# Weight sums of a Strassen-Winograd feed-forward: three VectorE operations a pair ahead instead of four GpSimd ones, and two products copied by ScalarE

## The chip, the cores and the metric

The kernel runs on one core of a Trainium2 chip. A core has TensorE (PE in the rows; its weight loads are PEld), VectorE (DVE), ScalarE (ACT), GpSimd (POOL) and SyncE (SP), which here issues nearly all DMAs. Each engine works through its own queue in order, and engines wait for each other on semaphores. The metric is the device time of one execution in microseconds, less being better, and the median of several runs is what is compared.

## The reference, cut to what matters

A decoder trunk of two layers, 512 tokens, width 1024. The change touches the four half-step feed-forwards alone (two in each layer, hidden width 2816):

```python
def swiglu_ffn(x, w_gu, w_down):
    gate, up = jnp.split(x @ w_gu, 2, axis=-1)
    return (jax.nn.silu(gate) * up) @ w_down
...
for i in range(DEPTH):
    x = x + 0.5 * swiglu_ffn(rmsnorm(x, ffn1_norm[i]), ffn1_w_gu[i], ffn1_w_down[i])
    x = x + Mixer_i(rmsnorm(x, mix_norm[i]))
    x = x + 0.5 * swiglu_ffn(rmsnorm(x, ffn2_norm[i]), ffn2_w_gu[i], ffn2_w_down[i])
```

All of it is float32. The kernel splits every operand in a rounded high part and a low part, and takes each product as high times high, high times low and low times high.

## The kernel before, in words

There are six stages: `f0a` (feed-forward), `ab` (a recurrent mixer), `f0b`, `f1a` (feed-forwards), `nsa` (an attention mixer) and `f1b` (feed-forward). Activations lie feature by token, eight tiles X[0..7] of 128 x 512, and all matmuls have a 128 x 128 weight block that stands still.

**A feed-forward** (`ffn`) has 22 hidden tiles of 128 units, each a *pair* of a gate tile and an up tile. The first four (`CLASSIC`) are taken in the plain way, from the gain-scaled but not yet normalised input `x` (`x phase` below): meanwhile the root mean square is found (`rms_sum`, `rms_row` give `Rcol`, then `R`), and `Quarters` makes the normalised input `xn` and from it seven combinations of its quarters, each split in high and low (`split`): B11, Q7, Q6 in `before()`, B21, Q4, Q5, B22 in `after()`. Their order is that of VectorE's queue.

The other 18 pairs use a Strassen-Winograd scheme, seven half-size products for eight: the gate and the up matrix of a hidden tile are a 2 x 2 block matrix (two halves of the 1024 features), the input another (two halves of the features by two halves of the tokens). `Pair.load` brings 1 MB of weights into two buffers `r` (`ra`, `rc`, four blocks of 128 x 512 each; two such sets, used in turn), forms the four sums of blocks that the scheme wants on GpSimd (lines 301 to 304), and splits the seven blocks in four *parts*: ScalarE copies the high part (`whi` or `wx`, line 310), VectorE subtracts for the low one (`wlo` or `wx`, line 311). There are five part buffers for four parts a pair. `Pair.p1` to `p7` are the products, 12 matmuls of 256 columns each, 84 a pair: product 1 and 7 start a sum in PSUM (`a`, `e`), later ones add on top of it, and after each of them ScalarE or VectorE takes out what stands there, before the next product changes it. In the order of TensorE's queue a pair is p1, p7, then p3 of the pair before, p6, p2, p4, p5. So p3, which adds into the same bank `a` as p5, comes 24 matmuls after p5, and must wait until VectorE has read what p5 left (line 355). `p3` also forms silu(gate) times up (line 362) and its split `h` (lines 380, 381).

Pairs come in groups of 4, 8 and 6 for lack of room for `h`; after each group the down projection (weights `wd`) adds into X. The two first pairs of a stage are interleaved: p.p1, p.p7, p.p6, q.p1, q.p7, p.p2, p.p4, p.p5 and so on.

**What sets the order.** TensorE's order is written out. On the other engines a scheduler places the instructions by priority: code under `tc.high_priority(offset=N)` counts as if written N instructions earlier. `SAHEAD` is the offset of a pair's loads, sums and splits, `EV` that of the PSUM reads, `AHEAD` that of the plainly used weights (`wload`). Once placed, a queue is never reordered when the program runs.

Of the kernel before, what the change touches and what calls it, by code (L numbers as in the profile page):

```python
# [12 lines left out]
P = 128  # L13
T = 512
# [10 lines left out]
SAHEAD = 230  # L25
EV = 320
# [27 lines left out]
def build(tc, a, out, stages=("f0a", "ab", "f0b", "f1a", "nsa", "f1b")):  # L54
    nc = tc.nc
    with ExitStack() as ctx:
# [182 lines left out]
        class Quarters:  # L239
# [12 lines left out]
            def split(self, name, src):  # L252
                t = blk(self.qb[QS.index(name)], F32R, f"q{name}")
                hi, lo = (t[:, n * 4 * H:(n + 1) * 4 * H].rearrange("p (k t) -> p k t", k=4) for n in range(2))
                nc.scalar.activation(hi, src, AF.Copy)
                nc.vector.tensor_sub(lo, src, hi.bitcast(F32))
                self.Q[name] = hi, lo

            def before(self):
                b11, b12, b21, b22 = self.f  # L260
                nc.vector.tensor_sub(b22, b12, b22)
                self.split("B11", b11)
                nc.gpsimd.tensor_sub(b12, b12, b11)
                self.split("Q7", b22)
                nc.vector.tensor_sub(b11, b11, b22)
                self.split("Q6", b11)

            def after(self):
                q6, q5, b21, b22 = self.f
                nc.gpsimd.tensor_add(b22, q5, q6)  # L270
                self.split("B21", b21)
                nc.vector.tensor_sub(b21, b21, q6)
                self.split("Q4", b21)
                self.split("Q5", q5)
                self.split("B22", b22)
# [12 lines left out]
        class Pair:  # L288
# [4 lines left out]
            def load(self, w, rb):  # L293
                with tc.high_priority(offset=SAHEAD):
# [3 lines left out]
                    nc.sync.dma_start(ra[:, 0:4:3], w[0].rearrange("p (s c) -> p s c", s=2))  # L298
                    nc.sync.dma_start(rc[:, 3], w[1][:, :T])
                    nc.sync.dma_start(rc[:, 0], w[1][:, T:])  # L300
                    nc.gpsimd.tensor_sub(ra[:, 1], rc[:, 3], ra[:, 0])  # L301
                    nc.gpsimd.tensor_add(rc[:, 1], rc[:, 0], rc[:, 3])
                    nc.gpsimd.tensor_sub(ra[:, 2], rc[:, 1], ra[:, 0])  # L303
                    nc.gpsimd.tensor_sub(rc[:, 2], ra[:, 3], ra[:, 2])
                    for src, names in ((ra[:, 0:2], ("B11", "Q7")), (ra[:, 2:4], ("Q6", "B21")),
                                       (rc[:, 0:2], ("Q4", "Q5")), (rc[:, 2:3], ("B22",))):
# [16 lines left out]
            def p1(self):  # L323
                self.a, self.t1 = psum(), tp.tile([P, T], F32, name="t1", bufs=3)
                self.product(self.a, "B11", True)
                with tc.high_priority(offset=EV):
                    nc.scalar.activation(self.t1[:, :H], self.a[:, :H], AF.Copy)

            def p2(self):
                b = psum()  # L330
                self.product(b, "B21", True)
                with tc.high_priority(offset=EV):
                    nc.vector.tensor_add(self.t1[:, :H], b[:, :H], self.t1[:, :H])
                nc.scalar.activation(self.t1[:, :H], self.t1[:, :H], AF.Silu)
# [17 lines left out]
            def p5(self):  # L352
                self.product(self.a, "Q5", False)
                with tc.high_priority(offset=EV):
                    nc.vector.tensor_add(self.t2[:, H:], self.a[:, :H], self.t2[:, H:])  # L355

            def p3(self):
                self.product(self.a, "B22", False)
                with tc.high_priority(offset=EV):
                    nc.scalar.activation(self.t1[:, H:], self.a[:, :H], AF.Silu)  # L360
# [4 lines left out]
        def ffn(gname, wgu, wd, x, lay, nxt, first=None):  # L365
# [30 lines left out]
            for j in range(CLASSIC):  # L396
                eng = nc.gpsimd if j > 1 else None
                (gh, gl), (uh, ul) = first if first and j == 0 else (wload(wgu[j, 0], eng=eng),
                                                                     wload(wgu[j, 1], eng=eng))
# [866 lines left out]
```

## Time and profile before

| | us |
|---|---|
| median of three runs | 2122.34 |
| lowest, highest | 2117.0, 2123.83 |
| the profiled execution | 2126.54 |
| its span, first to last instruction | 2124.8 |

The profile is of one execution, 4.2 us over the median; some 1.7 us of it lie outside the span. A row of the timeline has a start, a duration and, in square brackets, how long the engine had been idle and who ended that. Durations of neighbouring rows overlap by some 0.07 us, so that the cost of an instruction in a full queue is the distance between two starts. The clock column (PEclk) is the share of TensorE's 2.4 GHz that was granted; 0.5 is its lower level, 1.2 GHz.

### The profile page before, as it was taken

What the parts mean: (1) busy time and instruction counts of PE and PEld (TensorE: products, weight loads), DVE (VectorE), ACT (ScalarE), POOL (GpSimd) and SP (SyncE); (2) the same over time, 40 slices, a digit from 0 to 9 for tenths busy, and PEclk for the clock granted to TensorE, in tenths of its full rate; (3) what the DMA queues carried; (4) which work ended last, traced back from release to release, by engine and by line L of the source; (5) the groups of instructions that cost most, each with busy time, mean ns of one, the idle gap of its engine ahead of it and who ended that gap; (6) DMA issues with size and microseconds to landing.
All of it is one profiled execution on the core that took longest, in us unless ns stands there. A gap on an engine that the chain in (4) does not pass through costs nothing.

```text
span 2124.8 us, 30587 instructions
## 1 busy us (share of the span) xinstructions
PE 2019.0 (95%) x11896; PEld 1753.4 (83%) x11896; DVE 1432.3 (67%) x2021; ACT 1015.2 (48%) x1828; POOL 858.3 (40%) x602
## 2 busy tenths in 40 slices
PE   7999999989998999999999999999999989999997
PEld 5889889767787889898798989877777667889896
DVE  4957757488658759485866947443877778659474
ACT  4535436445544435254543525434877754435252
POOL 6425523243134427163433614202655554427152
PEclk8999999999899999999999999999999999999998
DMA  4233322222132323233232333321100032323212
GB/s 160 80 110 95 115 75 75 90 80 90 60 99 80 108 81 112 83 101 94 80 110 90 100 94 95 119 84 60 36 16 30 17 114 70 100 90 108 86 61 84
DMA packets 73585, 182.09 MB, mean 86 GB/s; under 512 B 7264, under 2 KB 8032, under 8 KB 73440
## 3 DMA queue, kind: packets, MB, share of 16 engines
q1 hardware_dynamic: 73296, 180.06, 26.7%
q8 instruction: 93, 1.52, 0.3%
q14 instruction: 52, 0.43, 0.1%
q10 hardware_dynamic: 144, 0.09, 0.0%
HBM read 178.02 MB, written 2.10 MB: 85 GB/s over the span
## 4 chain that ended last, share of the span: by engine, by line
PE 75%; DVE 12%; issue 4%; ACT 3%; POOL 3%; DMA 1%; SPq 0%; POOLq 0%; DVEq 0%; ACTq 0%
PE ps L174 18%; PE ps L175 18%; PE ps L176 18%; PE pt L175 3%; PE pt L176 3%; PE pt L174 3%; PE px L977 2%; PE pt L772 2%; DVE wx L311 1%; DVE wlo L169 1%; DMA r<-wgu 1%; PE pt L993 1%; DVE h L381 1%; DVE t L362 1%; DVE wlo L311 1%
## 5 line engine op out<-in xcount | busy, mean ns | idle before, releaser
L301 POOL TENSOR_TENSOR r<-r,r 128x512 f32<-128x512 f32 x72 | 124.0, 1723 | 627.7 <-DMA r<-wgu 587.8
L168 ACT ACTIVATE whi<-raw 128x1024 fp32r<-128x1024 f32 (+2 forms) x196 | 193.2, 987 | 368.9 <-PE ps L175 268.2
L175 PE MATMUL ps<-h,whi 128*128 128x512 f32 x704 | 277.2, 394 | 0.5 <-DVE h L381 0.5
L174 PE MATMUL ps<-h,whi 128*128 128x512 f32 x704 | 276.3, 393 | 0.9 <-ACT h L380 0.9
L176 PE MATMUL ps<-h,wlo 128*128 128x512 f32 x704 | 276.5, 393 | 0.0
L311 DVE TENSOR_TENSOR wlo<-r,whi 128x1024 fp32r<-128x1024 f32 (+1 forms) x174 | 237.2, 1365 | 50.3 <-ACT whi L310 48.9
L310 ACT ACTIVATE whi<-r 128x1024 fp32r<-128x1024 f32 (+1 forms) x174 | 165.5, 951 | 188.5 <-PE ps L175 129.4
L169 DVE TENSOR_TENSOR wlo<-raw,whi 128x1024 fp32r<-128x1024 f32 (+2 forms) x150 | 186.7, 1246 | 76.4 <-ACT whi L168 71.6
L450 DVE SCALAR_TENSOR_TENSOR X<-ps,X 128x512 f32<-128x512 f32 x96 | 66.4, 691 | 253.9 <-PE ps L176 253.9
L169 POOL TENSOR_TENSOR wlo<-raw,whi 128x1024 fp32r<-128x1024 f32 (+1 forms) x46 | 108.7, 2364 | 257.0 <-ACT whi L168 247.5
L311 DVE TENSOR_TENSOR wx<-r,wx 128x1024 fp32r<-128x1024 f32 (+1 forms) x114 | 170.2, 1493 | 57.5 <-ACT wx L310 57.1
L174 PE MATMUL ps<-x,whi 128*128 128x512 f32 x432 | 179.7, 416 | 0.4 <-ACT x L103 0.4
L174 PE MATMUL ps<-qB,whi 128*128 128x256 f32 x520 | 148.5, 286 | 25.0 <-DVE t L355 25.0
L176 PE MATMUL ps<-x,wlo 128*128 128x512 f32 x432 | 171.5, 397 | 0.0
L175 PE MATMUL ps<-x,whi 128*128 128x512 f32 x432 | 171.0, 396 | 0.3 <-DVE x L104 0.3
L175 PEld LDWEIGHTS ps<-h,whi 128*128 128x128 f32 x704 | 132.9, 189 | 31.0 <-DVE h L381 2.3
L174 PEld LDWEIGHTS ps<-h,whi 128*128 128x128 f32 x704 | 133.0, 189 | 30.7 <-ACT h L380 1.8
L176 PEld LDWEIGHTS ps<-h,wlo 128*128 128x128 f32 x704 | 132.8, 189 | 28.6
L115 POOL TENSOR_TENSOR acc<-acc,t 128x512 f32<-128x512 f32 x48 | 74.8, 1558 | 189.4 <-ACT t L113 178.3
L175 PE MATMUL ps<-qB,whi 128*128 128x256 f32 x520 | 146.4, 282 | 0.0
L176 PE MATMUL ps<-qB,wlo 128*128 128x256 f32 x520 | 146.4, 282 | 0.0
L303 POOL TENSOR_TENSOR r<-r,r 128x512 f32<-128x512 f32 x72 | 134.3, 1865 | 5.3
(341 smaller groups left out, 5897.7 us busy)
## 6 DMA issues: line engine op xcount, KB each, us to landing
r<-wgu SPq DMA_DIRECT2D x72, 512.0 KB, 3.9
r<-wgu SPq DMA_DIRECT2D x144, 256.0 KB, 2.8
raw<-wd SPq DMA_DIRECT2D x64, 512.0 KB, 3.5
raw<-wgu SPq DMA_DIRECT2D x30, 512.0 KB, 3.6
raw<-wd SPq DMA_DIRECT2D x32, 384.0 KB, 3.1
raw<-ab_fm SPq DMA_DIRECT2D x21, 512.0 KB, 3.5
raw<-nsa_fm SPq DMA_DIRECT2D x17, 512.0 KB, 3.5
raw<-ab_out SPq DMA_DIRECT2D x8, 512.0 KB, 3.6
```

The lines of the kernel that those rows point to most:

```text
L115: nc.gpsimd.tensor_add(acc, acc, sq)
L168: nc.scalar.activation(hi[:, :n], raw[:, :n], AF.Copy)
L169: (eng or nc.vector).tensor_sub(lo[:, :n], raw[:, :n], hi[:, :n].bitcast(F32))
L174: nc.tensor.matmul(ps, wh, xh, start=start, stop=False, skip_group_check=on)
L175: nc.tensor.matmul(ps, wh, xl, start=False, stop=False, skip_group_check=on)
L176: nc.tensor.matmul(ps, wl, xh, start=False, stop=stop, skip_group_check=on)
L301: nc.gpsimd.tensor_sub(ra[:, 1], rc[:, 3], ra[:, 0])
L303: nc.gpsimd.tensor_sub(ra[:, 2], rc[:, 1], ra[:, 0])
L310: nc.scalar.activation(hi[:, :m], src, AF.Copy)
L311: nc.vector.tensor_sub(lo[:, :m], src, hi[:, :m].bitcast(F32))
L450: nc.vector.scalar_tensor_tensor(X[i], ps, 0.5, X[i], op0=OP.mult, op1=OP.add)
L772: nc.tensor.matmul(p2[m][:, :155].rearrange("p (g n) -> p g n", g=5), w[:, q * 256 + m * P:q * 256 + (m + 1) * P], tt[:, :, n:n + 8 * 30 + ...
```

## The change

- The four sums of a pair become three, all additions, on VectorE: one of 128 x 1024 with an input that is repeated, and two of 128 x 512. Signs are put right elsewhere: the quarters B11, B21 and B22 are split from minus their value, and the silu takes scale -1.
- The loads of a pair (now four of 256 KB instead of one of 512 KB and two of 256 KB) and the sums get an offset of their own, `RAHEAD` = 400; the splits keep 230. The parts hold other names: B11 Q7, B21 Q6, Q5 Q4, B22.
- Two sums of the input quarters and the low parts of the classic weights of hidden tiles 2 and 3 go from GpSimd to VectorE too.
- Product 1 is copied by ScalarE into a second PSUM bank, product 2 adds on top of it, and the silu reads that bank: VectorE's addition after p2 is gone. Product 5 is copied by ScalarE into a tile `u4` (one buffer), and VectorE adds from there.

GpSimd keeps the sums of squares (`acc`) and its work in the two mixers.

```diff
+RAHEAD = 400
...
             def split(self, name, src):
...
-                nc.scalar.activation(hi, src, AF.Copy)
-                nc.vector.tensor_sub(lo, src, hi.bitcast(F32))
+                if name[0] == "B":
+                    nc.scalar.activation(hi, src, AF.Copy, scale=-1.0)
+                    nc.vector.scalar_tensor_tensor(lo, src, -1.0, hi.bitcast(F32), op0=OP.mult, op1=OP.subtract)
+                else:
+                    nc.scalar.activation(hi, src, AF.Copy)
+                    nc.vector.tensor_sub(lo, src, hi.bitcast(F32))
...
-                nc.gpsimd.tensor_sub(b12, b12, b11)
+                nc.vector.tensor_sub(b12, b12, b11)
...
-                nc.gpsimd.tensor_add(b22, q5, q6)
                 self.split("B21", b21)
                 nc.vector.tensor_sub(b21, b21, q6)
                 self.split("Q4", b21)
                 self.split("Q5", q5)
+                nc.vector.tensor_add(b22, q5, q6)
                 self.split("B22", b22)
...
             def load(self, w, rb):
-                with tc.high_priority(offset=SAHEAD):
+                with tc.high_priority(offset=RAHEAD):
...
-                    nc.sync.dma_start(ra[:, 0:4:3], w[0].rearrange("p (s c) -> p s c", s=2))
+                    nc.sync.dma_start(ra[:, 0], w[0][:, :T])
                     nc.sync.dma_start(rc[:, 3], w[1][:, :T])
-                    nc.sync.dma_start(rc[:, 0], w[1][:, T:])
-                    nc.gpsimd.tensor_sub(ra[:, 1], rc[:, 3], ra[:, 0])
-                    nc.gpsimd.tensor_add(rc[:, 1], rc[:, 0], rc[:, 3])
-                    nc.gpsimd.tensor_sub(ra[:, 2], rc[:, 1], ra[:, 0])
-                    nc.gpsimd.tensor_sub(rc[:, 2], ra[:, 3], ra[:, 2])
-                    for src, names in ((ra[:, 0:2], ("B11", "Q7")), (ra[:, 2:4], ("Q6", "B21")),
-                                       (rc[:, 0:2], ("Q4", "Q5")), (rc[:, 2:3], ("B22",))):
+                    nc.sync.dma_start(ra[:, 3], w[1][:, T:])
+                    nc.sync.dma_start(rc[:, 0], w[0][:, T:])
+                    nc.vector.tensor_add(ra[:, 1:3], ra[:, 0:4:3], rc[:, 3:4].to_broadcast([P, 2, T]))
+                    nc.vector.tensor_add(rc[:, 1], ra[:, 0], ra[:, 2])
+                    nc.vector.tensor_add(rc[:, 2], rc[:, 0], rc[:, 1])
+                with tc.high_priority(offset=SAHEAD):
+                    for src, names in ((ra[:, 0:2], ("B11", "Q7")), (rc[:, 0:2], ("B21", "Q6")),
+                                       (ra[:, 2:4], ("Q5", "Q4")), (rc[:, 2:3], ("B22",))):
...
             def p1(self):
-                self.a, self.t1 = psum(), tp.tile([P, T], F32, name="t1", bufs=3)
+                self.a, self.b, self.t1 = psum(), psum(), tp.tile([P, T], F32, name="t1", bufs=3)
                 self.product(self.a, "B11", True)
                 with tc.high_priority(offset=EV):
-                    nc.scalar.activation(self.t1[:, :H], self.a[:, :H], AF.Copy)
+                    nc.scalar.activation(self.b[:, :H], self.a[:, :H], AF.Copy)
             def p2(self):
-                b = psum()
-                self.product(b, "B21", True)
+                self.product(self.b, "B21", False)
                 with tc.high_priority(offset=EV):
-                    nc.vector.tensor_add(self.t1[:, :H], b[:, :H], self.t1[:, :H])
-                nc.scalar.activation(self.t1[:, :H], self.t1[:, :H], AF.Silu)
+                    nc.scalar.activation(self.t1[:, :H], self.b[:, :H], AF.Silu, scale=-1.0)
...
             def p5(self):
                 self.product(self.a, "Q5", False)
+                u4 = tp.tile([P, H], F32, name="u4", bufs=1)
                 with tc.high_priority(offset=EV):
-                    nc.vector.tensor_add(self.t2[:, H:], self.a[:, :H], self.t2[:, H:])
+                    nc.scalar.activation(u4, self.a[:, :H], AF.Copy)
+                    nc.vector.tensor_add(self.t2[:, H:], u4, self.t2[:, H:])
             def p3(self):
                 self.product(self.a, "B22", False)
                 with tc.high_priority(offset=EV):
-                    nc.scalar.activation(self.t1[:, H:], self.a[:, :H], AF.Silu)
+                    nc.scalar.activation(self.t1[:, H:], self.a[:, :H], AF.Silu, scale=-1.0)
...
-                eng = nc.gpsimd if j > 1 else None
-                (gh, gl), (uh, ul) = first if first and j == 0 else (wload(wgu[j, 0], eng=eng),
-                                                                     wload(wgu[j, 1], eng=eng))
+                (gh, gl), (uh, ul) = first if first and j == 0 else (wload(wgu[j, 0]), wload(wgu[j, 1]))
```

**VectorE, the start of the program.** In these rows `r0` and `r1` are a pair's buffers `ra` and `rc`, `raw` a block of plainly used weights, `X` and `x` the input and its low part, and the number is that of the tile. Before, from the first row that works on data, and then the rows around the root mean square (`ms`, `Rcol`):

```order
L104 SCALAR_TENSOR_TENSOR x2_96<-X0_70,prm_78,x0_94 128x512
L1127 TENSOR_TENSOR wlo_114<-raw_112,whi_113 128x128
L1127 TENSOR_TENSOR wlo_117<-raw_115,whi_116 128x128
...
L169 TENSOR_TENSOR wlo_238<-raw_235,whi_237 128x1024
L311 TENSOR_TENSOR wx4_555<-r0_546,wx4_555 128x1024
L169 TENSOR_TENSOR wlo_244<-raw_241,whi_243 128x1024
L311 TENSOR_TENSOR wx3_543<-r1_523,wx3_543 128x512
L142 TENSOR_SCALAR ms_268<-ps_263 128x4
```

The same two places of the change:

```order
L309 TENSOR_TENSOR r0_546<-r0_546,r1_547 128x1024
L309 TENSOR_TENSOR r0_522<-r0_522,r1_523 128x1024
L310 TENSOR_TENSOR r1_547<-r0_546 128x512
L310 TENSOR_TENSOR r1_523<-r0_522 128x512
L311 TENSOR_TENSOR r1_547<-r1_547 128x512
L311 TENSOR_TENSOR r1_523<-r1_523 128x512
L1134 TENSOR_TENSOR wlo_114<-raw_112,whi_113 128x128
...
L170 TENSOR_TENSOR wlo_238<-raw_235,whi_237 128x1024
L170 TENSOR_TENSOR wlo_244<-raw_241,whi_243 128x1024
L170 TENSOR_TENSOR wlo_362<-raw_359,whi_361 128x1024
L143 TENSOR_SCALAR ms_268<-ps_263 128x4
```

The sums of the first two pairs now stand ahead of all work on the input (and their eight loads ahead of the input's in SyncE's queue), and no split of a pair stands directly ahead of the root mean square any more.

**VectorE, within a group of pairs** (the eight-pair group of `f0a`). `wlo`, `wx` are low parts, `t2` the up half with its additions, `h` the split product. Before:

```order
L311 TENSOR_TENSOR wx3_1895<-r1_1879,wx3_1895 128x1024
L355 TENSOR_TENSOR t2_1794<-ps_1778,t2_1794 128x256
L311 TENSOR_TENSOR wx4_1898<-r1_1879,wx4_1898 128x512
L311 TENSOR_TENSOR wlo_2011<-r0_2001,whi_2010 128x1024
L311 TENSOR_TENSOR wlo_2015<-r0_2001,whi_2014 128x1024
L362 TENSOR_TENSOR t2_1794<-t1_1779,t2_1794 128x512
L333 TENSOR_TENSOR t1_1902<-ps_1960,t1_1902 128x256
```

Of the change:

```order
L364 TENSOR_TENSOR t2_1679<-u4_1760,t2_1679 128x256
L319 TENSOR_TENSOR wlo_1783<-r1_1764,whi_1782 128x512
L390 TENSOR_TENSOR h8_430<-t2_1555,h8_430 128x512
L319 TENSOR_TENSOR wlo_1897<-r0_1887,whi_1896 128x1024
L309 TENSOR_TENSOR r0_2011<-r0_2011,r1_2012 128x1024
L319 TENSOR_TENSOR wlo_1901<-r1_1888,whi_1900 128x1024
L310 TENSOR_TENSOR r1_2012<-r0_2011 128x512
L371 TENSOR_TENSOR t2_1679<-t1_1664,t2_1679 128x512
L311 TENSOR_TENSOR r1_2012<-r1_2012 128x512
L357 TENSOR_TENSOR t2_1803<-pt_1802,t2_1803 128x256
```

Line 355, the read of product 5 out of PSUM, is gone from this queue (line 364 reads `u4`), and line 309 stands in it three rows behind the last reader of the buffer that its own load refills: `r1_2012` takes the room of `r1_1764`.

**ScalarE at the same place.** Before, the end of a pair (product 5 isn't read here):

```order
L380 ACTIVATE h8_430<-t2_1671 128x512
L310 ACTIVATE wx3_1895<-r1_1879 128x1024
L334 ACTIVATE t1_1779<-t1_1779 128x256
L310 ACTIVATE wx4_1898<-r1_1879 128x512
L327 ACTIVATE t1_1902<-ps_1901 128x256
```

Of the change:

```order
L341 ACTIVATE t1_1788<-ps_1787 128x256
L318 ACTIVATE wx3_1904<-r1_1888 128x1024
L389 ACTIVATE h8_430<-t2_1679 128x512
L363 ACTIVATE u4_1884<-ps_1786 128x256
L318 ACTIVATE wx4_1907<-r1_1888 128x512
L336 ACTIVATE ps_1911<-ps_1910 128x256
```

The copy of product 5 (line 363) stands behind line 389, which waits for VectorE's line 371 of the pair before.

## Rows read from the trace of the kernel before

**Rows 1.** The page: busy time of an engine, share of the span, instructions.

```profile
PE 2019.0 (95%) x11896; PEld 1753.4 (83%) x11896; DVE 1432.3 (67%) x2021; ACT 1015.2 (48%) x1828; POOL 858.3 (40%) x602
```

**Rows 2.** Windows of the eight groups of 8 and 6 pairs: engines busy (instructions), PEclk, DMA.

```profile
164.30:248.50 84.20, 80.12 (x674) 79.47 (x673) 72.84 (x71) 47.20 (x78) 57.60 (x31) 0.99 0.32 101
...
sum 582.90, PE 559.45 PEld 554.54 DVE 480.96 ACT 323.27 POOL 352.13; mean PE 69.93 PEld 69.32 DVE 60.12 ACT 40.41 POOL 44.02
```

**Rows 3.** Windows of the first two pairs (168 matmuls) of each feed-forward.

```profile
675.20:704.40 29.20, 22.77 (x169) 22.12 (x168) 22.83 (x22) 14.99 (x23) 11.92 (x6) 0.88 0.26 85
...
sum 112.70, PE 90.08 PEld 87.50 DVE 90.68 ACT 61.50 POOL 45.73; mean PE 22.52 PEld 21.88 DVE 22.67 ACT 15.38 POOL 11.43
```

**Rows 4.** Windows: 40 us of a group without a TensorE wait, and 8 us with one.

```profile
200.00:240.00 40.00, 40.00 (x341) 39.79 (x340) 36.28 (x38) 24.39 (x41) 29.44 (x17) 1.00 0.33 106
939.00:947.00 8.00, 6.26 (x40) 6.05 (x39) 6.53 (x7) 3.74 (x7) 3.17 (x3) 0.79 0.20 67
```

**Rows 5.** Waits, TensorE: who was waited for, us in total, times, longest.

```profile
PE ps L174 <- DVE t L355: 33.1, 22, 3.9
PE pt L175 <- DVE qQ L256: 11.6, 4, 4.7
PE pt L149 <- DVE Rcol L130: 10.3, 2, 9.1
```

**Rows 6.** Timeline, TensorE, at product 4 of the first pair of f0b.

```profile
690.89 0.58 PE L175 MATMUL pt<-qQ,wx 128*128 128x256 f32 x1 [4.70 <-DVE qQ L256]
691.27 0.41 PE L176 MATMUL pt<-qQ,wx 128*128 128x256 f32 x1
691.49 0.41 PE L174 MATMUL pt<-qQ,wx 128*128 128x256 f32 x1
```

**Rows 7.** Timeline, VectorE, while GpSimd is idle: 128x512, 128x1024, then 128x256 from PSUM.

```profile
73.52 0.68 DVE L381 TENSOR_TENSOR h<-t,h 128x512 fp32r<-128x512 f32 x1
74.13 1.21 DVE L256 TENSOR_TENSOR qQ<-xn,qQ 128x1024 fp32r<-128x1024 f32 x1
75.26 1.21 DVE L256 TENSOR_TENSOR qB<-xn,qB 128x1024 fp32r<-128x1024 f32 x1
...
91.16 0.41 DVE L355 TENSOR_TENSOR t<-ps,t 128x256 f32<-128x256 f32 x1
91.49 0.68 DVE L311 TENSOR_TENSOR wlo<-r,whi 128x512 fp32r<-128x512 f32 x1
```

**Rows 8.** Timeline, VectorE, the same 128x1024 subtraction a little later.

```profile
84.92 2.28 DVE L256 TENSOR_TENSOR qQ<-xn,qQ 128x1024 fp32r<-128x1024 f32 x1
```

**Rows 9.** Timeline, GpSimd, its sums at that time.

```profile
83.99 2.13 POOL L303 TENSOR_TENSOR r<-r,r 128x512 f32<-128x512 f32 x1
```

**Rows 10.** Timeline, SyncE issues a freed buffer's load; GpSimd starts the sum of it.

```profile
92.19 0.34 SPq L299 DMA_DIRECT2D r<-wgu  x1
...
95.18 1.91 POOL L301 TENSOR_TENSOR r<-r,r 128x512 f32<-128x512 f32 x1 [6.83 <-DMA r<-wgu]
```

**Rows 11.** Windows at the start of the program: the input's loads, and a standstill.

```profile
5.00:10.00 5.00, 4.28 (x16) 3.23 (x16) 2.94 (x6) 4.41 (x10) 1.99 (x2) 1.00 1.00 318
...
35.00:40.00 5.00, 0.00 (x0) 0.00 (x0) 1.86 (x1) 1.73 (x3) 4.92 (x4) 0.78 0.00 0
```

**Rows 12.** Timeline, VectorE, around the first root mean square.

```profile
27.81 1.23 DVE L311 TENSOR_TENSOR wx<-r,wx 128x1024 fp32r<-128x1024 f32 x1 [9.59 <-ACT wx L310]
...
38.14 2.16 DVE L311 TENSOR_TENSOR wx<-r,wx 128x512 fp32r<-128x512 f32 x1 [6.87 <-ACT wx L310]
...
40.49 2.03 DVE L128 SCALAR_TENSOR_TENSOR rt<-Rcol 128x4 f32<-128x4 f32 x1
```

**Rows 13.** Timeline, SyncE, loads of the first two pairs at the start.

```profile
18.87 1.08 SPq L299 DMA_DIRECT2D r<-wgu  x2
```

**Rows 14.** Timeline, VectorE, f0b: first use of R, and the last split before product 4.

```profile
645.28 0.69 DVE L387 TENSOR_TENSOR t<-ps,R 128x512 f32<-128x512 f32 x1 [2.15 <-ACT R L151]
...
689.62 1.21 DVE L256 TENSOR_TENSOR qQ<-xn,qQ 128x1024 fp32r<-128x1024 f32 x1
```

## The prediction

> **What bounds the kernel now.** First the page's busy times [rows 1]: TensorE 95% busy, VectorE 67%, GpSimd 40%. A share over the whole span says little here, so the next view is the windows by stage. The eight groups of 8 and 6 pairs hold 4 x (672 + 504) = 4704 matmuls of 256 columns, and take 582.90 us together [rows 2]. What they would take without a wait is read from 40 us in which TensorE was never idle: 341 matmuls, 117.3 ns each, so 84 of them, a pair, take 9.85 us [rows 4]. 4704 x 117.3 ns = 551.8 us, so 31 us of these groups are lost, 0.56 us a pair. The first two pairs of the four feed-forwards take 112.70 us where 8 x 9.85 = 78.8 would do: 33.9 us lost [rows 3]. Eight more pairs, the rest of the groups of four, I take at the 0.56 us: 4.4 us. Beside the pairs there is a standstill at the start of the program, 35 to 40 us without a matmul [rows 11].
>
> The view of the waits names the causes [rows 5]. The largest, 33.1 us in 22 waits, is TensorE waiting for VectorE's line 355, the read of product 5, before it may add product 3 into the same bank. Then 11.6 us for the splits of the quarters (first pairs), 10.3 us for the first Rcol. A wait costs more than its length: behind the 4.70 us wait at 690.89 the matmuls start 0.22 us apart instead of 0.117 (691.27, 691.49), and over an 8 us window with such a wait the granted clock is 0.79, part of it the lower level of 1.2 GHz [rows 4, 6]. So the bound is TensorE, and what is to be had is about 70 us of waits behind VectorE's queue.
>
> **The change part by part.**
>
> *VectorE within a group.* Alone, a 128x1024 operation costs 1.13 us from start to start, a 128x512 one 0.61, a 256-wide read from PSUM 0.33 [rows 7]. A pair costs it now three splits of 1024 and one of 512, three PSUM reads, the product (line 362) and its split: 3 x 1.13 + 3 x 0.61 + 3 x 0.33 = 6.2 us. In the full window it is busy 36.28 of 40 us, and 40 / 9.85 = 4.06 pairs fit in, so it really needs 8.9 us a pair [rows 4]. The 2.7 us between are GpSimd's doing: the subtraction that lasts 1.21 us alone lasts 2.28 while GpSimd sums weights, and GpSimd's sums stretch as well [rows 7 to 9]. The change adds sums of 1.13 + 2 x 0.61 = 2.35 us and removes one PSUM read, 0.33; the addition from `u4` costs what line 355 cost. New need: 6.2 + 2.35 - 0.33 = 8.2 us, say 8.3 with the chain of the dependent sums. Below the 8.9 of now, and below TensorE's 9.85.
>
> But the sums bring a wait into VectorE's queue. Line 309 needs the loads that refill a buffer whose last reader stands three rows ahead of it. From the end of that reader (92.17) to the sum that GpSimd could start on the new data (95.18) it takes 3.0 us [rows 7, 10]. In the queue two operations stand between, 0.61 + 1.13 = 1.7 us of cover; at about half of the pairs there is only one of 1.13. So 1.3 to 1.9 us of standing, 1.6 taken, and a cycle of 8.3 + 1.6 = 9.9 us, level with TensorE's 9.85. Queued behind it are the split of the next pair (line 319) and line 371. Where VectorE runs ahead, its queue stands anyway at line 319 until TensorE frees a part buffer, and the load arrives in that time; so 9.9 holds only where it is late.
>
> *What TensorE waits for.* Product 3 now needs ScalarE's copy of product 5. ScalarE is busy 24.39 of 40 us [rows 4]. Its copy stands behind line 389, which needs line 371 of VectorE: the old dependence is not cut, it gets longer, but line 371 belongs to the pair before, and p3 comes 24 matmuls, 2.8 us, after p5. Followed through one pair of the new order with these durations, the copy ends some 1 us after p5, 1.7 us to spare. So most of the 31 + 4.4 us goes. I keep 0.15 us a pair for a VectorE as full as TensorE, 10 us over 64 pairs: **-25 us**. Bounds: all of it gone, -35; nothing gone, 0; a loss is the first rival.
>
> *The first two pairs of f0b, f1a, f1b.* From R to the split that product 4 waits for, VectorE's own work is now 25 operations of 512 and 13 of 1024, 25 x 0.61 + 13 x 1.13 = 30 us, and it took 45.5 us (645.28 to 690.8) [rows 14]; the rest is GpSimd and waits. In the new order 27 and 21 stand there (classic weights, quarter sums, two of the pair sums, splits of the next pair): 16.5 + 23.7 = 40.2 us, nothing of it stretched. With some 2 us for one load that line 309 waits for and for ScalarE's copies it is 42, 3.3 us earlier: 3 x 3.3 = **-10 us**. Each may be 5 us off: -25 to +5.
>
> *The start of the program.* Removed: VectorE stood at line 311 until GpSimd had made eight sums one after another (38.14), the root mean square stood behind that (one tiny step of it took 2.03 us beside GpSimd), and TensorE stood some 9 us [rows 5, 12], then ran at the lower clock. Added: eight loads, 2.1 MB, ahead of the input. SyncE takes 0.54 us for each [rows 13], 4.3 us, and at the 318 GB/s of the full queue [rows 11] they take 6.6 us; then VectorE makes both pairs' sums, 2 x 2.35 = 4.7 us, before it splits the first tile of the input, at some 13 us instead of 5.3. TensorE begins its second matmul 7 us later. But its first 48 matmuls were held up by the input's loads and splits anyway; laid out with the durations above, they end 2 to 3 us later than now, the third classic weight is split near 30 us, and Rcol follows at 31 us instead of 43. Sum: +3 for the late start, -9 for the wait, -2 for the clock behind it: **-8 us**. Bounds: -12, and +8 if the late start stays whole and Rcol, now behind that third weight's load, waits as long as before.
>
> *Group ends.* Before the down projection VectorE has also the next two pairs' sums in its queue, ahead of the last `h`. Now these ends cost next to nothing; 12 ends at 0.3 us, **+4 us** (0 to +12). The loads' new split, the signs and the second bank cost nothing: four issues of 0.54 us a pair in a queue that is otherwise idle, copies of the same size, one bank more of five, each bank free before its turn.
>
> Sum: -25 - 10 - 8 + 4 = -39 us on an execution of 2126.5 us (span 2124.8 and 1.7 outside), 2087; the profiled run is 4.2 us above the median of 2122.3, so the median becomes **2083 us**.
>
> **The rivals.**
>
> 1. *VectorE becomes the bound, slower.* In these groups a pair takes 582.9 / 56 = 10.41 us now, so the change loses there as soon as line 309 stands longer than 10.41 - 8.3 = 2.1 us a pair. If a late VectorE finds the loads always just issued, it stands the whole 3.0 us: 11.3 us a pair, 0.9 x 64 = +58 us, with the other terms 2122 + 58 - 14 = 2166; half way, 2140. For it: the cover is 1.1 to 1.7 us only [rows 7, 10]. Against: at 9.9 us there is 0.5 us to spare before the present pace. Here the Trainium skill speaks against the change: "Perfetto Trace Analysis", section "Optimizing Scalar/DVE Operations", advises to take work off a saturated VectorE, to ScalarE or even GpSimd, and adds that the shared read port may spoil the latter. By the first half alone the 2 us a pair that are added would be paid in full, 64 x 2 = 128 us, an estimate, about 2250; the row of 36.28 busy in 40 us agrees on the saturation, but rows 7 to 9 show the second half: GpSimd already takes more from VectorE (2.7 us a pair) than its sums will cost there.
>
> 2. *The wait only passes to ScalarE.* If VectorE runs 2 us late, line 371 holds line 389, and that the copy of product 5: p3 waits as before. The pairs gain nothing: -10 - 8 + 4 = -14, 2108. For it: the spare time is 1.7 us. Against: that needs VectorE late at most pairs.
>
> 3. *The late start stays.* +8 instead of -8: 2099. For it: all loads of the input now queue behind 2.1 MB. Against: the Rcol wait is two thirds GpSimd's sums, which are gone.
>
> 4. *A draw:* VectorE at 10.3 us and starts that gain nothing, about 2118.
>
> **How the numbers follow.** The forecast, 2060 to 2098: 0.55. Rival 2: 0.17, rival 3: 0.08, rival 4: 0.06, rival 1: 0.14. About 0.3%, 6.4 us, is what a measurement here can tell from no change: under 2116 is faster, so 0.55 + 0.17 + 0.08 = 0.80 faster, 0.06 the same, 0.14 slower. The range goes from all pair waits and most of the first pairs' gone (-25 to -35 in the groups, -25 at the first pairs, -12, 0: some 2050) up to 2128, which takes in rivals 2 to 4 and the mild end of the first.
>
> **What would show it.** In the profile after: no GpSimd row in the pair groups, and every 1024-wide VectorE row there at 1.2 us (else the 2.7 us were not GpSimd's); idle time before line 309 that ends by a load, 1.3 to 1.9 us where VectorE is late; TensorE's wait for product 5's read down from 33.1 us to under 10, now named after line 363; the eight groups' sum near 560 us; the first row of Rcol near 31 us, and the first split of the input near 13. Wrong if line 309 idles over 2 us at most pairs, if its repeated input makes it slower than 1.21 us, or if the splits of the first pairs come later than before.

## The result, and the profile after

The changed kernel takes 2097.2 us (median of 4 runs, 2094.8 to 2106.2) where the kernel before takes 2123.1: a ratio of 0.9886, 95% interval 0.9854 to 0.9917. That is faster by 26 us; 39 had been forecast, with a range of 2050 to 2128. A second measurement of the changed kernel, made later (below), gave 2105.2 us and 0.9921 [0.9907, 0.9935], so the gain is 18 to 26 us. The sign held and the time lies in the range, but it did not come from where the forecast had put it.

The profiled execution took 2106.2 us, span 2104.5, against 2126.5 and 2124.8 before; it lies 9 us above its own median, which matters below where traces are set against medians. The busy times of the page (columns as in [rows 1]):

```profile
PE 2014.4 (96%) x11896; PEld 1750.7 (83%) x11896; DVE 1383.4 (66%) x2189; ACT 1027.8 (49%) x1900; POOL 280.0 (13%) x290
```

GpSimd has lost 578 us of work. VectorE has 168 operations more and is nevertheless busy 49 us less. TensorE is about as busy as before, and the end moved by 20 us only. Where, the windows tell. The eight groups of 8 and 6 pairs, as [rows 2] (us; PE, PEld, DVE, ACT, POOL busy; granted clock; DMA share):

```profile
158.60:244.40 85.80, 80.34 (x674) 79.70 (x673) 65.67 (x87) 48.00 (x86) 0.00 (x0) 0.98 0.30 92
...
sum 587.70, PE 562.69 PEld 557.27 DVE 434.84 ACT 330.20 POOL 1.55; mean PE 70.34 PEld 69.66 DVE 54.36 ACT 41.28 POOL 0.19
```

587.7 us against 582.9: nothing was won here, where the forecast had put most of the 25 us of its largest term, although VectorE's busy time fell from 481 to 435 us. The groups of four pairs, with which each feed-forward begins, take 183.3 us against 199.5 (matmuls from the first to the last; their first two pairs 100.9 against 112.8), and the first of them begins at 66.4 instead of 71.5. The first two pairs of f0b, as [rows 3], where the kernel before took 29.20 us:

```profile
668.80:695.00 26.20, 22.64 (x170) 22.11 (x169) 18.69 (x22) 13.30 (x22) 0.00 (x0) 0.87 0.14 41
```

TensorE's waits, as [rows 5]:

```profile
PE ps L175 <- ACT u L363: 14.5, 12, 3.1
PE pt L175 <- ACT qQ L261: 8.2, 3, 3.6
PE ps L177 <- DVE wx L319: 7.5, 6, 1.5
...
PE ps L176 <- DVE x L105: 4.9, 3, 1.7
PE pt L176 <- DVE qQ L262: 4.8, 4, 1.5
PE ps L175 <- ACT t L352: 4.6, 2, 3.1
```

The 33.1 us behind product 5 [rows 5] have become 14.5, under the name of ScalarE's copy, and beside them stand new waits for splits of the weights (`wx`) and for the copy of product 6 (line 352). And in the page's costliest groups (busy, mean ns of one, then idle time before and its releaser) there is a row that did not exist:

```profile
L309 DVE TENSOR_TENSOR r<-r,r 128x1024 f32<-128x1024 f32 x72 | 89.4, 1242 | 130.5 <-DMA r<-wgu 130.4
```

VectorE stands 130 us in front of the first sum of a pair, for a load. One such case on VectorE (start, length; in brackets the idle time before and what ended it):

```profile
204.06 1.23 DVE L309 TENSOR_TENSOR r<-r,r 128x1024 f32<-128x1024 f32 x1 [2.50 <-DMA r<-wgu]
...
209.95 0.68 DVE L319 TENSOR_TENSOR wx<-r,wx 128x512 fp32r<-128x512 f32 x1
210.55 0.68 DVE L390 TENSOR_TENSOR h<-t,h 128x512 fp32r<-128x512 f32 x1
211.15 1.22 DVE L319 TENSOR_TENSOR wlo<-r,whi 128x1024 fp32r<-128x1024 f32 x1
214.90 1.23 DVE L309 TENSOR_TENSOR r<-r,r 128x1024 f32<-128x1024 f32 x1 [2.53 <-DMA r<-wgu]
```

and SyncE's issues of the loads meanwhile:

```profile
209.72 0.33 SPq L305 DMA_DIRECT2D r<-wgu  x1
210.09 0.43 SPq L307 DMA_DIRECT2D r<-wgu  x1
210.66 0.34 SPq L306 DMA_DIRECT2D r<-wgu  x1
211.04 0.43 SPq L308 DMA_DIRECT2D r<-wgu  x1
```

The split at 209.95 is the last reader of the pair's second buffer. SyncE issues its loads as soon as it ends (210.63). Behind it VectorE has 1.7 us of work, then it stands 2.53 us until the load of line 306 is there, 4.2 us after its issue. From one line 309 to the next are 10.84 us, 8.31 of work and 2.53 of standing, where TensorE needs 9.85 for a pair [rows 4].

### The profile page after: what moved, and what is told of

Read it like the earlier page. It is cut to its first block, busy times and chain, and to the rows that moved or that the text cites. A ratio compares the mean times of both kernels' runs of the same rounds, so it can differ in the third digit from the quotient of the medians.

```text
span 2104.5 us, 30561 instructions
## 1 busy us (share of the span) xinstructions
PE 2014.4 (96%) x11896; PEld 1750.7 (83%) x11896; DVE 1383.4 (66%) x2189; ACT 1027.8 (49%) x1900; POOL 280.0 (13%) x290
## 4 chain that ended last, share of the span: by engine, by line
PE 72%; DVE 12%; DMA 6%; issue 5%; ACT 3%; POOL 0%; SPq 0%; DVEq 0%; POOLq 0%; ACTq 0%
PE ps L175 17%; PE ps L176 17%; PE ps L177 17%; DMA r<-wgu 6%; PE pt L176 3%; PE pt L175 3%; PE pt L177 3%; PE px L984 2%; PE pt L779 2%; DVE wlo L319 1%; PE pt L1000 1%; DVE wx L319 1%; DVE r L309 1%; DVE r L310 1%; PE ps L944 1%
## 5 line engine op out<-in xcount | busy, mean ns | idle before, releaser
L170 DVE TENSOR_TENSOR wlo<-raw,whi 128x1024 fp32r<-128x1024 f32 (+2 forms) x166 | 192.5, 1162 | 78.7 <-ACT whi L169 73.8
L457 DVE SCALAR_TENSOR_TENSOR X<-ps,X 128x512 f32<-128x512 f32 x96 | 66.4, 691 | 238.1 <-PE ps L177 238.1
L319 DVE TENSOR_TENSOR wlo<-r,whi 128x1024 fp32r<-128x1024 f32 (+1 forms) x174 | 189.1, 1088 | 28.1 <-ACT whi L318 27.8
L309 DVE TENSOR_TENSOR r<-r,r 128x1024 f32<-128x1024 f32 x72 | 89.4, 1242 | 130.5 <-DMA r<-wgu 130.4
L319 DVE TENSOR_TENSOR wx<-r,wx 128x1024 fp32r<-128x1024 f32 (+1 forms) x114 | 125.1, 1098 | 23.6 <-ACT wx L318 21.1
L389 ACT ACTIVATE h<-t 128x512 fp32r<-128x512 f32 x88 | 55.4, 630 | 145.3 <-DVE t L371 143.1
L318 ACT ACTIVATE wx<-r 128x1024 fp32r<-128x1024 f32 (+1 forms) x114 | 107.5, 943 | 11.4 <-DVE r L309 9.1
```

Of the source, the lines that this page charges most:

```text
L170: (eng or nc.vector).tensor_sub(lo[:, :n], raw[:, :n], hi[:, :n].bitcast(F32))
L309: nc.vector.tensor_add(ra[:, 1:3], ra[:, 0:4:3], rc[:, 3:4].to_broadcast([P, 2, T]))
L318: nc.scalar.activation(hi[:, :m], src, AF.Copy)
L319: nc.vector.tensor_sub(lo[:, :m], src, hi[:, :m].bitcast(F32))
L389: nc.scalar.activation(hh, t2, AF.Copy)
L457: nc.vector.scalar_tensor_tensor(X[i], ps, 0.5, X[i], op0=OP.mult, op1=OP.add)
```

## Experiments

Each kernel was timed in three rounds or more beside the kernel before, whose median lay between 2120.3 and 2123.9 us in these sessions; of two kernels from different sessions a difference of some 3 us is therefore not shown. The theory after the first look was that the groups' gain was lost at line 309, and nowhere else; its rivals were ScalarE's copy of product 5 (rival 2 of the prediction) and that VectorE has simply too much to do.

**Line 309 later in the queue.** A one-column copy out of the third split of the pair before, into the place that line 309 overwrites, puts line 309 behind that split. Nothing else changes in the code; the scheduler places the rest of VectorE's queue anew around it.

```diff
-            def load(self, w, rb):
+            def load(self, w, rb, prev=None):
...
+                    if prev is not None:
+                        nc.vector.tensor_copy(ra[:, 1, 0:1], prev.W["Q5"][1][:, 0:1].bitcast(F32))
                     nc.vector.tensor_add(ra[:, 1:3], ra[:, 0:4:3], rc[:, 3:4].to_broadcast([P, 2, T]))
```

> Edit: line 309 of a pair is put later in VectorE's queue, behind the split of products Q5 and Q4 of the pair before (a one-column copy out of that split into the place line 309 overwrites, 0.06 to 0.16 us a pair); loads and all else as in the changed kernel (2097 us). Between the last reader of the buffer and line 309 there now lie some 5 us of VectorE's work instead of 1.1 to 1.7. Theory A (the gain of the groups was lost at line 309, where a load takes 4.3 us from the buffer's release to the sum): VectorE's idle time before line 309 falls from 130 us to under 40, the eight groups from 588 us to about 563, the time to 2070 to 2078. Theory B (ScalarE's copy of product 5 holds product 3, whatever line 309 does): the idle time goes, but TensorE's wait for the copy stays at 10 to 15 us and the groups above 580, time 2090 to 2098. Theory C (VectorE's sums are simply too much work): the idle time moves to other lines, time 2095 to 2105.

Measured: 2040.8 us (2039.1 to 2045.6), 0.9623 [0.9602, 0.9645]: 56 us under the changed kernel's first median and 64 under its second, more than theory A had said. The windows of the eight groups, their sum, and below it the page's row for line 309 (here line 311):

```profile
sum 551.40, PE 550.20 PEld 549.39 DVE 454.72 ACT 340.14 POOL 1.79; mean PE 68.78 PEld 68.67 DVE 56.84 ACT 42.52 POOL 0.22
```

```profile
L311 DVE TENSOR_TENSOR r<-r,r 128x1024 f32<-128x1024 f32 x72 | 89.0, 1238 | 14.2 <-DMA r<-wgu 12.5
```

The eight groups take 551.4 us; the prediction had put what TensorE needs without a wait at 551.8. TensorE is busy in 550.2 of them, with VectorE busier in them than in the changed kernel (454.7 us against 434.8). So neither theory B nor C: the sums on VectorE fit, and ScalarE's copy holds nobody, once no load is waited for. Theory A had said 563 for these groups, and it had not counted the 20 us that came in the groups of four pairs (163.5 us against 183.3).

**A smaller dose.** The same copy, but out of `t2` of the pair three ahead, which leaves 3.1 us of work and more between the last reader and the sum (`prev.t2[:, H:H + 1]`, from the fourth pair on).

> Edit: as in the first run, but line 309 is put only behind line 371 of the pair three ahead: some 3.1 us of VectorE's work between the buffer's last reader and line 309, where the changed kernel has 1.1 to 1.7 and the first run (2040.8 us) 5.7. From release to sum the changed kernel took 3.9 us on average (62 pairs). Theory A (the price is the load's time less the cover, and TensorE waits only for what lifts the cycle over its 9.85 us): 0.8 us of idle time before line 309 a pair, 55 to 75 us in all instead of 130, a cycle of 8.0 + 0.8 = 8.8 us, under TensorE's, so nearly the whole gain: 2041 to 2050. Rival D (the first run gained by another order of the splits, not by the load's cover): no graded answer, 2060 to 2097.

Measured: 2059.9 us (2057.7 to 2060.8), 0.9723 [0.9706, 0.9739], between the two forecasts and at the edge of the second; so the time alone does not decide. The page's row says more:

```profile
L311 DVE TENSOR_TENSOR r<-r,r 128x1024 f32<-128x1024 f32 x72 | 89.9, 1249 | 33.7 <-DMA r<-wgu 32.6
```

33.7 us are left before the sum, less than the 55 forecast, and the eight groups take 552.1 us, as short as with the full dose. The groups of four take 179.5 us: their gain needs the third pair's sums late, which this edit does not touch. The eight groups thus gain by the cover, as theory A says. Rival D, another order of the splits, isn't excluded by this, since every such edit reorders VectorE's queue; the quarter loads below, which leave that order nearly as it was, exclude it.

**Only the third pair late.** The first edit with `prev = q` for the third pair alone.

> Edit to the changed kernel: only the third pair of each feed-forward has line 309 put late (as the first run had for all pairs). If the first run's gain has two parts that add (20 us in the groups of four pairs, where the third pair's sums stood ahead of the quarters' last splits, and 36 us in the eight later groups): the groups of four pairs as short as in the first run (163.6 us together), the eight at 588, 2074 to 2081. If the groups of four need all sums late: 2085 to 2097.

Measured: 2086.1 us (2083.9 to 2093.0), 0.9837 [0.9811, 0.9864]. The time is 5 us above the first forecast and inside the second, but the trace bears out the first: the two parts add, the groups of four take 165.1 us (163.5 with all late), the eight others 589.1, and the groups of four do not need all sums late. From trace to trace the edit took 20.9 us off the span, from median to median 11. To see which of the two differences is right the changed kernel was measured again.

> The changed kernel itself once more, since its profiled run (2106.2 us) lay 9 us above its median (2097.2), and the run before this one (third pair late) took 21 us off the span of the profiled execution but 11 us off the median. If the median of 2097 is right: 2094 to 2100, and the third pair's sums late are worth 11 us. If the profiled run was the typical one: 2101 to 2107, and they are worth 15 to 20.

Measured: 2105.2 us (2103.6 to 2109.4). So the changed kernel varies between 2095 and 2109 us, its two traces (spans 2104.5 and 2104.3) stand for the upper half, and the third pair's sums are worth 11 to 19 us.

What these sums held up is read in the changed kernel: VectorE's queue at the start of f0b's pairs (the third pair's sums are lines 309 to 311), and then the two matmuls of TensorE that waited for it:

```profile
668.34 1.22 DVE L309 TENSOR_TENSOR r<-r,r 128x1024 f32<-128x1024 f32 x1
...
670.08 0.69 DVE L310 TENSOR_TENSOR r<-r 128x512 f32<-128x512 f32 x1
...
671.81 0.69 DVE L311 TENSOR_TENSOR r<-r 128x512 f32<-128x512 f32 x1
...
680.43 1.22 DVE L262 TENSOR_TENSOR qQ<-xn,qQ 128x1024 fp32r<-128x1024 f32 x1
```

```profile
679.93 0.58 PE L175 MATMUL pt<-qQ,wx 128*128 128x256 f32 x1 [2.36 <-ACT qQ L261]
681.71 0.58 PE L176 MATMUL pt<-qQ,wx 128*128 128x256 f32 x1 [1.20 <-DVE qQ L262]
```

The third pair's sums, 2.3 us, are made ahead of the quarter's split for which product 4 stands 3.6 us at 679.93 and 681.71. The next matmuls start 0.21 us apart, the lower clock of [rows 6].

**Why the load took so long.** From the last reader's end to the sum (release to sum) it took 3.9 us on average (62 pairs of the changed kernel) against 2.9 before (64 pairs). It is the load itself that comes later, not the sum behind it: from issue to landing the awaited load takes 3.8 us in the median and took 2.6 before (72 each). The trace suggests the company it is in: in 32 pairs the later of the first buffer's two loads had been issued 0.6 to 1.2 us before, so that four loads of 256 KB were under way together, and the one awaited took 4.2 us from its issue to the sum; the six times that VectorE waited and they had been issued over 4 us before, it took 2.6. To test that, the first buffer's two loads bring a quarter of their columns from the third pair on (`ra[:, 0, :T // 4]`, `ra[:, 3, :T // 4]`), so that this part of the feed-forwards isn't computed. For that each set's first buffer stays one tile through a whole feed-forward.

> Edit to the changed kernel: from the third pair of a feed-forward on, the two loads into the first buffer of a pair bring a quarter of their columns (64 KB instead of 256 KB each; the other three quarters keep an older pair's weights, so this part of the feed-forwards isn't computed). VectorE's order stays as in the changed kernel, and so do the two loads into the second buffer, one of which line 309 waits for. Theory A1 (the load takes 3.9 us instead of the 2.9 of the kernel before because four loads of 256 KB are in flight together): release to sum falls to 2.6 to 3.0 us, the idle time before line 309 from 130 us to 60 to 80, the eight groups from 588 us to 555 to 570, the time from 2097 to 2060 to 2080. Rival (VectorE's own way of waiting costs the extra us, or the issues on SyncE do): no change, 2092 to 2100.

Measured: 2060.1 us (2055.1 to 2062.7), 0.9703 [0.9682, 0.9725]. Release to sum falls to 3.1 us (63 pairs; here VectorE often comes later than the load), issue to landing to a median of 2.6, the sum's row to

```profile
L312 DVE TENSOR_TENSOR r<-r,r 128x1024 f32<-128x1024 f32 x72 | 89.3, 1242 | 60.9 <-DMA r<-wgu 60.4
```

and the eight groups to 553.2 us; the groups of four, 178.4, get 5 us shorter. That is theory A1: the extra microsecond was the company of the first buffer's loads, and not VectorE's way of waiting or SyncE's issue. Whether it was their bytes alone isn't shown, for the tile that is kept also moves one of them: it is issued 6.7 us before the awaited load in the median, instead of 1.6 (the other 1.6 instead of 1.2). The load that line 309 waits for was the same, and VectorE's order nearly so (of its 2189 operations some 60 stand elsewhere), so the gain of the eight groups did not need another order of the splits (rival D). The Trainium skill ("DMA: Bandwidth & Descriptors", section "Anatomy of one DMA — SWDGE (gpsimd) path") gives a load a fixed part of some 2.0 us and one that goes with its bytes; its fit is for loads issued from GpSimd, and for 256 KB it makes 2.6 us, an estimate. The six loads whose first buffer had long been served took just that; that a load takes 4.2 in closer company doesn't follow from the size of one.

**Product 5 read by VectorE again**, in the changed kernel and in the one with the late sums:

```diff
-                u4 = tp.tile([P, H], F32, name="u4", bufs=1)
...
-                    nc.scalar.activation(u4, self.a[:, :H], AF.Copy)
-                    nc.vector.tensor_add(self.t2[:, H:], u4, self.t2[:, H:])
+                    nc.vector.tensor_add(self.t2[:, H:], self.a[:, :H], self.t2[:, H:])
```

> Edit: VectorE reads product 5 from its bank again, as in the kernel before, and ScalarE's copy of it is gone; the sums stay on VectorE. Theory A (line 309): product 5's read still stands behind line 309, now directly in VectorE's queue, so the wait of TensorE for it stays at 14 us or grows to 30; time 2095 to 2112. Theory B (ScalarE's copy): that wait, 14.5 us, falls under 5 and the time to 2083 to 2088.

Measured on the changed kernel: 2109.8 us (2109.6 to 2111.0), 0.9946 [0.9927, 0.9965], 5 to 13 us lost. TensorE's first wait:

```profile
PE ps L175 <- DVE t L362: 26.4, 25, 3.6
```

Without ScalarE's copy product 3 waits for VectorE's read again, 26.4 us (33.1 before the change).

> Edit: the first run (line 309 late), with product 5 read by VectorE from its bank again. On the changed kernel the same edit cost 12.6 us (2109.8). If ScalarE's copy only let product 3 pass a VectorE that stood at line 309: with that wait gone it costs nothing, 2038 to 2044. If the copy relieves VectorE's queue as such: 8 to 13 us lost, 2049 to 2054.

Measured with late sums: 2041.2 us (2038.7 to 2042.3), the same as the 2040.8 with the copy, and no wait for product 5's read is left among TensorE's longest. So the copy is worth something only as a way around a VectorE that stands in front of a load.

**The sums back on GpSimd**, four of 128x512 in the new formulas, all else as changed (`nc.gpsimd.tensor_add` in place of lines 309 to 311).

> Edit: the four weight sums of 128x512 back on GpSimd, in the new kernel's formulas; ScalarE's copies, classic weights and quarter sums stay as in the changed kernel. Theory A: line 309's wait leaves VectorE, but the splits beside GpSimd's sums stretch again from 1.2 to 1.5 us and more; the two nearly cancel in the eight groups (575 to 588 us), the first pairs and the program start lose part of their gain; time 2092 to 2110. If the stretching of VectorE had cost nothing: groups near 560 and 2070. If the gain of the first pairs were due to the classic weights and quarter sums alone: first two pairs of f0b, f1a, f1b as short as in the changed kernel.

Measured: 2099.8 us (2097.9 to 2110.4), 0.9908 [0.9877, 0.9939]: not to be told from the changed kernel. VectorE no longer waits for a load, and what it pays instead stands in the page:

```profile
L320 DVE TENSOR_TENSOR wlo<-r,whi 128x1024 fp32r<-128x1024 f32 (+1 forms) x174 | 246.8, 1425 | 43.1 <-ACT whi L319 42.6
```

A split takes 1425 ns on average beside GpSimd's sums and 1088 in the changed kernel, the same operations. The eight groups are 22 us shorter than in the changed kernel (565.7, below the 575 expected), but the down projections 9 us longer (500.8 against 492.0) and the groups of four 7 (189.9). Moving the sums to VectorE was a draw, because the wait for the load ate the contention that it removed.

**Classic weights and quarter sums back on GpSimd** (the `eng` of `wload` for j > 1, and two sums of the quarters).

> Edit to the changed kernel: the splits of the third and fourth classic weight pairs, and two of the quarter sums, back on GpSimd; the pairs' weight sums and the copies stay as changed. If the first pairs gained by these leaving GpSimd: the groups of four pairs of f0b, f1a, f1b get 4 to 6 us longer each, back to before's 48 to 52 us, the eight other groups stay at 588, time 2107 to 2115. If they gained by the weight sums leaving GpSimd (or by ScalarE's copies): no change, 2094 to 2100.

Measured: 2111.7 us (8 runs, 2108.8 to 2115.6), 0.9962 [0.9947, 0.9976]. The groups of four take 196.4 us, 13.1 more, and nothing else moved by more than 5. This part of the change is what shortened the first pairs.

**The start of the program.** The first two pairs' loads and sums behind the input, by giving them the splits' offset (230) in f0a.

> Edit: the eight loads and the sums of the first two pairs of the program stand behind the input's loads and splits in their queues, as in the kernel before; else the changed kernel. If the late start costs what the trace suggests: first split of the input at 5.3 us instead of 13.7, second matmul near 6 instead of 14.5, Rcol's first row near 31 instead of 36, and the time 4 to 7 us less, 2090 to 2093. If VectorE, busy from 8.6 to 29 us, has the same work before Rcol anyway: Rcol at 35 to 36 and no change, 2095 to 2099.

Measured: 2094.6 us (2090.9 to 2097.4), 0.9868 [0.9843, 0.9892]; against medians of 2097.2 and 2105.2 that is a gain of 3 to 11 us. The trace shows it: the first split of the input stands at 5.07 us, the first row of Rcol comes at 34.80 (40.77 in the changed kernel), and the first pair begins at 60.5 instead of 66.4.

**Both together.** Late sums and the start behind the input.

> Edit: the first run (2040.8 us) with the first two pairs' loads and sums of the program behind the input's, which took 2.6 us off the changed kernel's median and 5.9 off its start in the trace. If the two gains are independent: 2035 to 2039. If the earlier start only runs into a later wait: 2040 to 2042.

Measured: 2037.9 us (2033.6 to 2042.6), 0.9628 [0.9606, 0.9650] of the kernel before. That is the ratio of late sums alone (0.9623), so the times show no gain of the start on top of it; the 3 us between the two medians are no more than the kernel before moved between these sessions. The trace has the first pair at 60.0 instead of 66.0.

## Why the prediction was right, and where it was wrong

The sign and the range held, but in part by luck: the term that carried 25 of the 39 us brought nothing, and 7 of the 20 us between the two traces come from stretches that the forecast had not named.

*The pair groups, -25 us: wrong; measured +5 (582.9 to 587.7).* The term also held the eight pairs left in the groups of four, which took 82.4 us instead of 86.7, so that all 64 pairs together come out even. The failed step is "it takes 3.0 us" from the reader's end to the sum. It was read from GpSimd's sum in the kernel before [rows 10], and there it is right. But the edit that the prediction put at no cost, the loads' and splits' new layout, changes it. The products Q5 and Q4 now lie in the first buffer, so that it is freed by the third split and not by the second. Its loads were issued long before the other's in the kernel before (none in the 8 us ahead of [rows 10]); now the later of them is issued 0.6 to 1.2 us before them at half of the pairs, and from release to sum it takes 3.9 us instead of 2.9. The cover of 1.1 to 1.7 us was read correctly. 3.9 less 1.7 is 2.2, and 2.2 us is the mean of the 45 waits before line 309 inside the eight groups (98.9 us), 30 of them over the 2.1 us from which, by the prediction's own sum, the change loses in these groups. That was rival 1, and here it came true in its mildest form. VectorE's own need was sized rightly: between one line 309 and the next in these groups it works 8.3 us (median of 37 such stretches), and a 1024-wide split of the weights lasts 1.22 us on average. With the standing such a stretch lasts 10.8 us on average, 29 of the 37 over TensorE's 9.85, where the forecast had 9.9.

*That VectorE's contention with GpSimd costs more than the sums: right.* The sums back on GpSimd show the price, 0.34 us a split on average, and the late sums the gain once the wait is gone. Here the Trainium skill ("Perfetto Trace Analysis", section "Optimizing Scalar/DVE Operations") had advice on both sides, off a saturated VectorE, and beware of GpSimd's shared port. The traces bear out the second half: 168 operations more, 49 us less busy.

*"Most of the waits for product 5 go": half right.* They fell from 33.1 to 14.5 us and not under 10, under the name that was foreseen, and the new waits beside them made up the rest. Rival 2, that the wait passes to ScalarE, names what the 14.5 us were, but not a cause: with late sums it makes no difference who reads product 5.

*The first pairs, -10 us: right in kind.* In f0b, f1a and f1b the first two pairs gained 3.2, 7.9 and 1.2 us, 12.3 together. Taken back to GpSimd, the classic weights and quarter sums cost just these groups 13 us, so it was they. But the prediction counted two of the pair sums into VectorE's work ahead of product 4 and did not ask whether they must stand there. They need not: the third pair's, put late, gave back another 11 to 19 us.

*The start, -8 us: -5.1.* The first split of the input at 13.66 us was foreseen (13); but the late start, put at 3 us, gave 5.9 in the trace when it was taken away. VectorE in the changed kernel, from its first sum on:

```profile
8.57 2.36 DVE L309 TENSOR_TENSOR r<-r,r 128x1024 f32<-128x1024 f32 x2 [7.57 <-DMA r<-wgu]
...
13.66 0.75 DVE L105 SCALAR_TENSOR_TENSOR x<-X,prm,x 128x512 fp32r<-128x512 f32 x1
...
19.05 3.46 DVE L105 SCALAR_TENSOR_TENSOR x<-X,prm,x 128x512 fp32r<-128x512 f32 x2
22.43 1.77 DVE L1134 TENSOR_TENSOR wlo<-raw,whi 128x512 fp32r<-128x512 f32 x1
24.12 4.76 DVE L105 SCALAR_TENSOR_TENSOR x<-X,prm,x 128x512 fp32r<-128x512 f32 x4
```

A split of the input takes 0.75 us at 13.66 and 1.7 us at 19.05, while GpSimd works from 16.84 to 27.01 us without a break, on squares and one split; at 27.48 it takes 0.74 again. In the kernel before, the same eight splits end at 16.0 us; pushed later, they met GpSimd. That is a piece of rival 3: Rcol's first row came at 40.77 and not at 31. TensorE's stop of 9 us [rows 5] is gone all the same (1.2 us are left).

*Group ends, +4 us: about right.* The down projections take 492.0 us against 489.2. *Not foreseen:* the stretches before f0b and f1b, -2.4 and -4.3 us.

In the traces this makes +5 (the eight groups), -16 (groups of four), -5 (the start), +3 (group ends) and -7, -20 us in all, against the -39 forecast. By experiments the change's three parts are worth, each taken back alone from the changed kernel: the classic weights and quarter sums 6 to 15 us, the copy of product 5 5 to 13 (against the medians 2105.2 and 2097.2), the pair sums nothing that can be told. Why the changed kernel itself came out at 2097 and at 2105 us in two sessions stays open.

## What to carry to other kernels

When work moves from one queue to another, the wait that it brings has to be priced in the new queue and with the new traffic: what is freed when, how many loads are then under way, and how much work lies between the release and the first use. In this kernel the same three sums on VectorE were worth nothing that can be told with 1.1 to 1.7 us of cover, and 56 us more (from 2097.2 to 2040.8) with some 5.7, against 3.9 us from release to sum. By the traces 36 of these came in the eight groups, by the cover, and 20 in the groups of four, most of them because the third pair's sums no longer stood ahead of the quarters' splits. Where an engine has time to spare and still stands, look first whether the waiting operation can stand later in its queue.

## What the runs showed of the hardware

- The time of a load of 256 KB went with what else was in flight: 2.6 us from issue to use with the other buffer's loads over 4 us old, 4.2 with the later of them 0.6 to 1.2 us old, and the median from issue to landing fell from 3.8 to 2.6 us when those others carried a quarter of their bytes and one of them was issued 5 us earlier.
- VectorE's splits of the pair weights (128x1024 and 128x512 together), 1088 ns on average with no weight sums on GpSimd, took 1425 ns with GpSimd's sums beside them; a 128x512 split of the input took 0.75 us with GpSimd idle and 1.7 beside its sums of squares.
- One and the same program (the changed kernel) gave medians of 2097.2 and 2105.2 us in two sessions, with the kernel before at 2123.1 and 2123.4. What is told from trace to trace needs the median beside it.
